# The first two projections of a hybrid trunk made side by side, from weights stored in the order of their use

## The chip, the cores and the metric

The kernel runs on one core of a Trainium2 chip. The metric is device time in microseconds; three runs of the kernel before took 2539.45, 2540.48 and 2542.24 us (median 2540.48). PE is TensorE (products), PEld its loads of weights, DVE is VectorE, ACT ScalarE, POOL GpSimd; SP is the engine that issues transfers.

## What is computed

The reference is a trunk of two layers on 256 tokens of width 2048: differential attention and a gated MLP with a short convolution, then a gated delta rule and a second MLP. The change touches the start of the attention:

```python
h = rms_norm(x, mixer_norm[0])
qkv = h @ w_qkv                      # 2048 x (2048 q, 2048 k, 2048 v)
q = rms_norm(q.reshape(..., 16, 128), q_norm) * 128 ** -0.5
k = rms_norm(k.reshape(..., 16, 128), k_norm)
...                                  # 8 heads, each of two halves of 128
```

All is float32, and must stay close to it.

## The kernel before

Everything lies transposed: `x` is 16 tiles of 128 features by 256 tokens (k = 0 to 15). A float32 number is carried as a sum of two parts that PE multiplies fast, hi (rounded to float32r) and lo (the rest). `weights` (line 75) fetches a piece of a weight matrix into a buffer `raw` (the transfer is issued by SP), ACT casts it to `whi` (line 86) and DVE subtracts to get `wlo` (line 87). There are four buffers of each, with room for 128 x 1024 numbers. `norm_tile` (line 184) makes the activations of one k likewise: ACT multiplies by the gain and rounds (line 189), DVE makes the rest (line 190). The division by the norm comes later, from a sum of squares, `norm_stat`.

`dense` (line 98) makes one block: 256 columns of the output, as two column tiles of 128, over all 16 k. It fetches 4 k at a time (512 KB); for each k and column tile it issues a pair of products: hi of the weights with both parts of the activations (512 wide, line 117) and lo of the weights with hi of the activations (256 wide, line 118). A block of 16 k is thus 32 pairs. It accumulates in one large PSUM tile `ps` of two banks per column tile pair; there are two such tiles, `banks`, and four small tiles of a bank each, `mp`.

`attention` (line 348) makes a block of q and a block of k for each of eight heads, in turn: q of head 0, k of head 0, q of head 1, and so on. The first block is special: its activations don't exist yet, so `start` (line 971) makes them as they are asked for, and issues the transfers of x on the way, and its first piece holds a single k (`lead`). A block of q or k is merged from its two parts out of PSUM by `normed` (line 387, `merge` at 143), and background work (sums of squares, statistics, weights of the attention, written as generators) goes forward by one step at each `tick`, that is after each piece. A scheduler then moves instructions of each engine past each other where no data forbid it.

Ahead of all this stand 18 products of a 128 x 128 tile of ones with itself (line 953), whose result is not used. The gains come by a transfer of their own (line 940).

Of the kernel before, what the change touches and what calls it, by code (L numbers as in the profile page):

```python
# [8 lines left out]
F32 = mybir.dt.float32  # L9
# [12 lines left out]
CK = 4  # L22
WARM = 18
LNEXP = "natural_log_exp_and_others"


class Trunk:
# [8 lines left out]
    def __init__(self, ctx, tc):  # L36
# [37 lines left out]

    def weights(self, ap):

        nc = self.nc
        nk, n = ap.shape[1:]

        def tile_(tag, dt, bufs):  # L80
            t = self.wp.tile([P, CK * T], dt, tag=tag, name=tag, bufs=bufs)
            return t[:, :nk * n].rearrange("p (k n) -> p k n", n=n)

        raw, hi, lo = tile_("raw", F32, 4), tile_("whi", F32R, 4), tile_("wlo", F32R, 4)
        self.loaded = nc.sync.dma_start(raw, ap)
        self.cast = nc.scalar.copy(hi, raw)  # L86
        nc.vector.tensor_tensor(lo, raw, hi.bitcast(F32), ALU.subtract)  # L87
        return hi, lo

    def chunks(self, kt, ck, first=0):  # L90

        c = [(k, min(ck, kt - k)) for k in range(0, kt, ck)]
        return [(0, first), (first, c[0][1] - first)] + c[1:] if first else c

    def banks(self):
        return self.dps.tile([P, 2, 2 * T], F32, tag="ps", name="ps")

    def dense(self, w, kt, acts, tiles=2, lead=0, wide=True, each=None):
# [6 lines left out]
        for k0, nk in self.chunks(kt, CK, lead):  # L105
            hi, lo = self.weights(w[:, k0:k0 + nk, :])
# [14 lines left out]
            self.tick()  # L121
        return ps

# [19 lines left out]
    def merge(self, ps, u, pool=None, scaled=True):  # L143

        nc = self.nc
        n = u.shape[1]
        main, small = self.halves(ps[:, :n])
        v = "p c (q j) -> p c q j"
# [198 lines left out]

    def attention(self, w_qk, w_v, w_o, nh, dist_ap, ident_ap, qg, kg, lvec, sub, start, done, lambda_init):

        nc, mp = self.nc, self.mp  # L350
        with self.tc.tile_pool(name="at", bufs=1) as at:
            self.spawn(self.norm_stat(4, at))
            qgs = at.tile([P, 1], F32, tag="qgs", name="qgs")
# [7 lines left out]
            def prepare():  # L361
                for _ in range(5):
                    yield
# [104 lines left out]
            for h in range(nh):  # L468
                acts, lead = (self.h_acts, 0) if h else (start, 1)
                qn, go = normed(self.dense(w_qk[h], KD, acts, lead=lead), qgs)  # L470
                self.spawn(go)
                kn, go = normed(self.dense(w_qk[nh + h], KD, self.h_acts), kg)
# [393 lines left out]
def _layout(inputs):  # L866
# [30 lines left out]
    for t, n in ((0, P), (1, T)):  # L897
# [8 lines left out]
        np.concatenate([_tiles(x["ffn_conv_w"][i].reshape(-1)), _tiles(x["ffn_conv_b"][i])], 1).reshape(P, 4, 2, NJ)  # L906
        for i in range(2)]
    def turned(w):
        return w.reshape(*w.shape[:-1], T, 2).swapaxes(-1, -2).reshape(w.shape)

    out = {
        "x": x["x"][0].T.reshape(KD, P, T).transpose(1, 0, 2),
        "cols": np.concatenate(col, 1),
        "w_qk": blocks(x["diff_w_qkv"][0], KD, pairs(2 * NH)),
        "w_v": turned(blocks(x["diff_w_qkv"][0], KD, [[(2 * NH * T + T * h, 2 * T)] for h in range(0, NH, 2)])),
# [18 lines left out]
def trunk_kernel(tc, a, out):  # L934
    nc = tc.nc
    with ExitStack() as ctx:
        t = Trunk(ctx, tc)
        n = a["cols"].shape[1]
        cols = t.cp.tile([P, n], F32, tag="cols", name="cols")
        nc.sync.dma_start(cols[:, :KD], a["cols"][:, :KD])  # L940
        parts = t.chunks(KD, CK, 1)

        def load():
            if parts:
                k, n = parts.pop(0)
                nc.sync.dma_start(t.x[:, k:k + n, :], a["x"][:, k:k + n, :])

# [4 lines left out]
        for _ in range(WARM):  # L952
            nc.tensor.matmul(warm[:, :P], t.onesr, t.onesr, start=True, stop=True)

# [16 lines left out]
        def start(k):  # L971

            if len(begun) <= k:
                if k == 0 or k in starts:
                    load()
                if k == KD - 1:
                    with tc.issue_after(t.loaded.ins):
                        nc.sync.dma_start(cols[:, KD:], a["cols"][:, KD:])
                then(mixer, 0)(k)
                begun.append(k)  # L980
            return t.h[k]

        t.attention(a["w_qk"], a["w_v"], a["w_o"], NH, a["dist"], a["const"][:, :P], qg, kg, lvec, sub, start, then(ffn, 0),
                    0.8 - 0.6 * math.exp(-0.3 * 0))
# [20 lines left out]
```

## Time and profile before

| | |
|---|---|
| median of three runs | 2540.48 us |
| the profiled execution | 2540.85 us |
| its span, first to last instruction | 2539.0 us |
| PE busy | 2530.1 us |
| DVE, ACT, POOL busy | 1899.5, 1506.3, 91.5 us |
| read from memory | 482.31 MB, 191 GB/s over the span |

A row of a timeline gives the start (us from the start of the span), how long it took, the engine, the line of the kernel, the operation, what it writes and reads, the shape, and in brackets how long the engine stood idle ahead of it and what ended that. A row of waits gives who waited for whom, us in total, times, and the longest. Products overlap: one that is listed with 0.38 us may be followed by the next after 0.22 us, so the distance between starts is the measure.

### The profile page before, as it was taken

The numbers are of one execution on the slowest core, as the hardware profiler recorded it, in microseconds if no ns is written. First come the engines' busy times: TensorE is split into PE (matmuls) and PEld (weight loads), VectorE is DVE, ScalarE is ACT, GpSimd is POOL, SyncE is SP. The second block draws the span as 40 slices with busy tenths as digits, with TensorE's granted clock in tenths as the row PEclk, the third lists the DMA queues.
The fourth block names the chain that finished last, engine by engine and source line by source line (L and its number), as shares of the span: only waits on it lengthen the run. The fifth ranks groups of instructions, "written<-read, shape, count | busy, mean of one in ns | idle before, by whom it ended". The sixth has DMA issues, their size and how long they took to land.

```text
span 2539.0 us, 44069 instructions
## 1 busy us (share of the span) xinstructions
PE 2530.1 (100%) x17442; PEld 2360.4 (93%) x17442; DVE 1899.5 (75%) x2787; ACT 1506.3 (59%) x2073; POOL 91.5 (4%) x189
## 2 busy tenths in 40 slices
PE   9999999999999999999999999999999999999999
PEld 8998899999999999999999999999999999999998
DVE  8876678777777555689878788788787777776544
ACT  7666556666666444485674674674566666665443
POOL 0000000000000000010121011021000000000000
PEclk9999999999999999999999999999999999999999
DMA  7555566666666666666555555555466666666665
GB/s 246 176 183 176 170 201 201 202 200 201 201 201 201 201 199 201 203 189 200 164 168 191 165 183 176 175 182 177 159 200 201 202 201 200 201 201 207 207 208 156
DMA packets 137775, 487.33 MB, mean 192 GB/s; under 512 B 15552, under 2 KB 18784, under 8 KB 137568
## 3 DMA queue, kind: packets, MB, share of 16 engines
q1 hardware_dynamic: 137280, 484.16, 60.5%
q8 instruction: 137, 2.24, 0.4%
q14 instruction: 70, 0.57, 0.1%
q10 hardware_dynamic: 288, 0.35, 0.0%
HBM read 482.31 MB, written 2.15 MB: 191 GB/s over the span
## 4 chain that ended last, share of the span: by engine, by line
PE 99%; DMA 1%; DVE 0%; ACT 0%; SPq 0%; issue 0%
PE ps L117 48%; PE ps L118 27%; PE ps L120 7%; PE ps L175 3%; PE ps L176 3%; PE ps L177 3%; PE mp L700 2%; PE mp L117 1%; PE mp L284 1%; PE mp L573 1%; PE mp L118 0%; PE mp L665 0%; PE mp L683 0%; PE mp L745 0%; PE mp L451 0%; PE mp L421 0%
## 5 line engine op out<-in xcount | busy, mean ns | idle before, releaser
L87 DVE TENSOR_TENSOR wlo<-raw,whi 128x1024 fp32r<-128x1024 f32 (+2 forms) x909 | 1103.1, 1215 | 520.3 <-ACT whi L86 512.1
L86 ACT CAST whi<-raw 128x1024 fp32r<-128x1024 f32 (+2 forms) x909 | 944.2, 1040 | 867.8 <-PE ps L117 558.1
L117 PE MATMUL ps<-h,whi 128*128 128x512 f32 (+1 forms) x4304 | 1361.6, 357 | 1.4 <-ACT whi L86 1.4
L118 PE MATMUL ps<-h,wlo 128*128 128x256 f32 x4304 | 1179.5, 274 | 0.6 <-DVE wlo L87 0.6
L117 PEld LDWEIGHTS ps<-h,whi 128*128 128x128 f32 x4304 | 819.7, 190 | 87.0 <-ACT whi L86 2.0
L118 PEld LDWEIGHTS ps<-h,wlo 128*128 128x128 f32 x4304 | 827.7, 192 | 2.5 <-DVE wlo L87 1.4
L117 PE MATMUL ps<-ac,whi 128*128 128x512 f32 x1546 | 506.8, 382 | 0.0
L118 PE MATMUL ps<-ac,wlo 128*128 128x256 f32 x1546 | 421.5, 273 | 0.0
L117 PEld LDWEIGHTS ps<-ac,whi 128*128 128x128 f32 x1546 | 293.1, 190 | 40.1 <-PE ps L117 0.2
L118 PEld LDWEIGHTS ps<-ac,wlo 128*128 128x128 f32 x1546 | 297.0, 192 | 0.1
L120 PE MATMUL ps<-h,whi 128*128 128x256 f32 x1040 | 287.5, 277 | 0.0
L120 PEld LDWEIGHTS ps<-h,whi 128*128 128x128 f32 x1040 | 199.9, 192 | 0.4
L175 PE MATMUL ps<-whi,h 128*128 128x512 f32 x384 | 146.4, 381 | 0.0
L177 PE MATMUL ps<-whi,h 128*128 128x512 f32 x384 | 146.2, 381 | 0.0
L176 PE MATMUL ps<-wlo,h 128*128 128x512 f32 x384 | 146.2, 381 | 0.0
L265 DVE SCALAR_TENSOR_TENSOR cv<-u,fcols,cv 128x255 f32<-128x255 f32 (+1 forms) x344 | 142.7, 477 | 0.0
L117 PE MATMUL ps<-oc,whi 128*128 128x256 f32 x512 | 142.5, 278 | 0.0
L120 PE MATMUL ps<-oc,whi 128*128 128x256 f32 x512 | 142.1, 278 | 0.0
L118 PE MATMUL ps<-oc,wlo 128*128 128x256 f32 x512 | 141.7, 277 | 0.0
L120 PEld LDWEIGHTS ps<-oc,whi 128*128 128x128 f32 x512 | 98.3, 192 | 0.3
L118 PEld LDWEIGHTS ps<-oc,wlo 128*128 128x128 f32 x512 | 98.4, 192 | 0.2
L117 PEld LDWEIGHTS ps<-oc,whi 128*128 128x128 f32 x512 | 98.4, 192 | 0.1
(208 smaller groups left out, 2151.2 us busy)
## 6 DMA issues: line engine op xcount, KB each, us to landing
raw<-w_up SPq DMA_DIRECT2D x344, 512.0 KB, 4.8
raw<-w_down SPq DMA_DIRECT2D x160, 512.0 KB, 3.8
raw<-w_in SPq DMA_DIRECT2D x128, 512.0 KB, 4.6
raw<-w_z SPq DMA_DIRECT2D x64, 512.0 KB, 4.0
raw<-w_out SPq DMA_DIRECT2D x64, 512.0 KB, 4.2
raw<-w_qk SPq DMA_DIRECT2D x63, 512.0 KB, 4.6
raw<-w_v SPq DMA_DIRECT2D x32, 512.0 KB, 3.9
raw<-w_o SPq DMA_DIRECT2D x32, 512.0 KB, 4.7
```

Source lines behind the costliest of these rows:

```text
L86: self.cast = nc.scalar.copy(hi, raw)
L87: nc.vector.tensor_tensor(lo, raw, hi.bitcast(F32), ALU.subtract)
L117: nc.tensor.matmul(bank[c][:, :n], hi[:, k, s], self.turns(a[:, :n // T, :]), start=first, stop=False)
L118: nc.tensor.matmul(bank[c][:, :T], lo[:, k, s], self.turns(a[:, :1, :]), start=False, stop=last and wide)
L120: nc.tensor.matmul(bank[c][:, :T], hi[:, k, s], self.turns(a[:, 1:, :]), start=False, stop=last)
L175: nc.tensor.matmul(ps[:, c, :], ah, wh, start=first, stop=False)
L176: nc.tensor.matmul(ps[:, c, :], ah, wl, start=False, stop=False)
L177: nc.tensor.matmul(ps[:, c, :], al, wh, start=False, stop=last)
L265: nc.vector.scalar_tensor_tensor(out[:, j:], u[:, :T - j], taps[n - 1 - j], out[:, j:], ALU.mult, ALU.add)
L284: last = self.nc.tensor.matmul(out, self.onesr, self.pairs(p[:, j]), start=i + j == 0, stop=i + j == n)
L573: nc.tensor.matmul(p[:, P:384], k[:, :P], r, start=True, stop=True)
L700: nc.tensor.matmul(p[:, v, :], l(v), r[:, v, :], start=i == 0, stop=i == len(terms) - 1)
```

## The change

Four things are changed, all at the start.

**The first two blocks side by side.** `dense_two` makes q and k of head 0 together in the two large PSUM tiles: for each k four pairs, two for q and two for k, so each activation is used at once for both. Their weights are stored anew, as `w_first`: for k = 0 to 11 the columns of q and k stand next to each other, 512 for each k, behind them the last four k of q, and the last four of k. They come in pieces of one k for k = 0 to 3 (two such pieces share one buffer), of two k up to 11, and then the last quarter of each block. The piece of k = 0 is cast in two halves.

**Transfers.** x comes in eight pieces of two k in place of five; the gains are stored in front of x, in one tile with it, and come with its first piece.

**The products of ones.** Seven in place of 18, each 512 wide in place of 128 (the tile of ones is read four times over).

**The third block.** q of head 1 goes into two small PSUM tiles in place of a large one (`apart`), and is merged in two halves. The statistics of the norm are begun after 8 steps of the background in place of 4, the small constants after 10 in place of 5.

```diff
-WARM = 18
+WARM = 7
...
-        self.x = self.cp.tile([P, KD, T], F32, tag="x", name="x")
+        self.gx = self.cp.tile([P, KD + KD * T], F32, tag="x", name="x")
+        self.x = self.gx[:, KD:].rearrange("p (k t) -> p k t", t=T)
...
+    def weights(self, ap, parts=1, slots=None, at=0):
...
+        for i in range(parts):
+            s = slice(i * n // parts, (i + 1) * n // parts)
+            self.cast = nc.scalar.copy(hi[:, :, s], raw[:, :, s])
+            nc.vector.tensor_tensor(lo[:, :, s], raw[:, :, s], hi[:, :, s].bitcast(F32), ALU.subtract)
...
+    def firsts(self):
+        return [(k, 1) for k in range(4)] + self.chunks(KD, 2)[2:]
+
+    def dense_two(self, w, acts, done):
+        ps = [self.banks(), self.banks()]
+        cut = KD - CK
+        parts = [(c, (0, 1)) for c in self.firsts() if c[0] < cut] + [((cut, CK), (b,)) for b in range(2)]
+        at = 0
+        for (k0, nk), bs in parts:
+            for k in range(nk):
+                acts(k0 + k)
+            n = len(bs) * T
+            ap = w[:, at:at + nk * n].rearrange("p (k n) -> p k n", n=n)
+            at += nk * n
+            if nk == 1 and k0 % 2 == 0:
+                slots = self.slots()
+            hi, lo = self.weights(ap, 1 if k0 else 2, slots if nk == 1 else None, k0 % 2 * 2 * T if nk == 1 else 0)
+            for i, b in enumerate(bs):
+                for c in range(2):
+                    s = slice(i * T + c * P, i * T + (c + 1) * P)
+                    for k in range(nk):
+                        a = acts(k0 + k)
+                        first, last = k0 + k == 0, k0 + k == KD - 1
+                        nc.tensor.matmul(ps[b][:, c, :], hi[:, k, s], self.turns(a), start=first, stop=False)
+                        nc.tensor.matmul(ps[b][:, c, :T], lo[:, k, s], self.turns(a[:, :1, :]), start=False, stop=last)
+                if k0 == cut:
+                    done[b](ps[b])
+            self.tick()
...
-        ps = self.banks() if each is None else None
-        bank = [self.mp() if each else ps[:, c] for c in range(tiles)]
+        ps = None if each or apart else self.banks()
+        bank = [ps[:, c] if ps else self.mp() for c in range(tiles)]
...
+        if isinstance(ps, list):
+            for c in range(2):
+                k = slice(c, c + 1)
+                main, small = self.halves(ps[c].unsqueeze(1))
+                nc.scalar.copy(t[:, k].rearrange(v, q=2), small)
+                nc.vector.tensor_tensor(u[:, k].rearrange(v, q=2), main, t[:, k].rearrange(v, q=2), ALU.add)
...
-            self.spawn(self.norm_stat(4, at))
+            self.spawn(self.norm_stat(8, at))
...
-                for _ in range(5):
+                for _ in range(10):
...
-        nc.sync.dma_start(cols[:, :KD], a["cols"][:, :KD])
-        parts = t.chunks(KD, CK, 1)
+        parts = t.chunks(KD, 2)
...
-            nc.tensor.matmul(warm[:, :P], t.onesr, t.onesr, start=True, stop=True)
+            nc.tensor.matmul(warm, t.onesr, t.onesr.unsqueeze(1).to_broadcast([P, 4, P]), start=True, stop=True)
```

The order of the instructions shows three places. First the transfers that SP issues from the start of the program, before (x_76 is x, each raw a weight buffer; the shapes are those in SBUF):

```order
L940 DMA cols_81<-cols 128x16
L946 DMA x_76<-x 128x256
L85 DMA raw_113<-w_qk 128x256
L946 DMA x_76<-x 128x768
L85 DMA raw_127<-w_qk 128x768
L946 DMA x_76<-x 128x1024
L85 DMA raw_152<-w_qk 128x1024
```

and now:

```order
L1003 DMA x_76<-x 128x528
L86 DMA raw_104<-w_first 128x512 x2
L1003 DMA x_76<-x 128x512
L86 DMA raw_137<-w_first 128x512 x2
L1003 DMA x_76<-x 128x512
L86 DMA raw_169<-w_first 128x1024
L1003 DMA x_76<-x 128x512
L86 DMA raw_196<-w_first 128x1024
```

For each k now 256 KB of weights come with 128 KB of x, where before it was 128 with 128; the small transfer of the gains is gone from the head of the queue.

Second the work of ACT over the same stretch, before:

```order
L189 ACTIVATE h_77<-x_76,cols_81 128x256
L86 CAST whi_114<-raw_113 128x256
L189 ACTIVATE h_77<-x_76,cols_81 128x256 x3
L86 CAST whi_128<-raw_127 128x768
L189 ACTIVATE h_77<-x_76,cols_81 128x256 x4
L86 CAST whi_153<-raw_152 128x1024
```

and now, up to the piece of k = 10 and 11 (raw_250):

```order
L234 ACTIVATE h_77<-x_76 128x256 x2
L89 CAST whi_105<-raw_104 128x256 x2
L89 CAST whi_105<-raw_104 128x512
...
L89 CAST whi_138<-raw_137 128x512 x2
...
L89 CAST whi_170<-raw_169 128x1024
...
L89 CAST whi_197<-raw_196 128x1024
...
L89 CAST whi_224<-raw_223 128x1024
L234 ACTIVATE h_77<-x_76 128x256 x6
L89 CAST whi_251<-raw_250 128x1024
```

Two activations stand ahead of each of the pieces up to k = 9, then the last six stand together ahead of the cast of k = 10 and 11.

Third, on PE, where the third block (q of head 1) begins, before (ps_255 is the tile of the second block, ps_380 that of the third):

```order
L117 MATMUL ps_255<-h_77,whi_351 128x512
L117 MATMUL ps_380<-h_77,whi_382 128x512
L118 MATMUL ps_255<-h_77,wlo_352 128x256
...
L118 MATMUL ps_380<-h_77,wlo_383 128x256
L117 MATMUL ps_380<-h_77,whi_382 128x512
```

and now (ps_101 is the tile of k of head 0, mp_349 and mp_350 the two small tiles):

```order
L124 MATMUL ps_101<-h_77,wlo_317 128x256
L151 MATMUL mp_349<-h_77,whi_352 128x512
L151 MATMUL mp_350<-h_77,whi_352 128x512
L419 MATMUL mp_413<-lp_96,ones_72 128x2
L152 MATMUL mp_349<-h_77,wlo_353 128x256
L152 MATMUL mp_350<-h_77,wlo_353 128x256
```

The third block begins behind the whole of the second, and the small product for lambda (L374 before, L419 now) has moved from the middle of the first block to the head of the third.

More of the change, by code (lines that the diff above doesn't have):

```diff
@@ L73, in tick, with slots @@
                 self.bg.remove(g)
-    def weights(self, ap):
+    def slots(self):
+        return [self.wp.tile([P, CK * T], dt, tag=tag, name=tag, bufs=4)
+                for tag, dt in (("raw", F32), ("whi", F32R), ("wlo", F32R))]
+    def weights(self, ap, parts=1, slots=None, at=0):
         nc = self.nc
         nk, n = ap.shape[1:]
[L80 to L84, printed above, removed]
+        raw, hi, lo = (t[:, at:at + nk * n].rearrange("p (k n) -> p k n", n=n) for t in slots or self.slots())
@@ L907, in _layout @@
         for i in range(2)]
+    qk = blocks(x["diff_w_qkv"][0], KD, [[(T * (h + i), T)] for h in range(NH) for i in (0, NH)])
+    two, cut = qk[:2], KD - CK
     def turned(w):
```

53 lines of the change are left out of this document (33 added, 20 removed).

## The prediction, made before the changed kernel ran

> **What bounds the kernel now.** The page comes first: the busy times and the chain that ended last.
>
> ```profile
> span 2539.0 us, 44069 instructions
> PE 2530.1 (100%) x17442; PEld 2360.4 (93%) x17442; DVE 1899.5 (75%) x2787; ACT 1506.3 (59%) x2073; POOL 91.5 (4%) x189
> PE 99%; DMA 1%; DVE 0%; ACT 0%; SPq 0%; issue 0%
> ```
>
> PE is busy for 2530.1 of 2539.0 us. An edit can only gain by taking products away, by running them at a higher clock, or by closing the few holes. The view of waits, for PE over the whole span, says where the holes are:
>
> ```profile
> PE mp L284 <- DVE qp L277: 1.5, 1, 1.5
> PE ps L117 <- ACT whi L86: 1.4, 1, 1.4
> PE mp L953 <- DVE onesr L54: 1.3, 1, 1.3
> PE ps L118 <- DVE wlo L87: 0.6, 2, 0.4
> ```
>
> All but the first (in the delta-rule stage, which the change doesn't touch) lie in the first 14 us. There the timeline of PE shows a second loss that no wait shows:
>
> ```profile
> 1.31 4.10 PE L953 MATMUL mp<-onesr 128*128 128x128 f32 x18 [1.31 <-DVE onesr L54]
> 5.95 0.64 PE L117 MATMUL ps<-h,whi 128*128 128x512 f32 x1
> 8.25 0.80 PE L117 MATMUL ps<-h,whi 128*128 128x512 f32 x1 [1.45 <-ACT whi L86]
> ...
> 9.61 0.64 PE L117 MATMUL ps<-h,whi 128*128 128x512 f32 x1
> 10.25 0.64 PE L117 MATMUL ps<-h,whi 128*128 128x512 f32 x1
> ...
> 11.96 0.31 PE L118 MATMUL ps<-h,wlo 128*128 128x256 f32 x1
> ...
> 13.19 0.38 PE L118 MATMUL ps<-h,wlo 128*128 128x256 f32 x1 [0.37 <-DVE wlo L87]
> ...
> 31.44 0.38 PE L117 MATMUL ps<-h,whi 128*128 128x512 f32 x1
> 31.77 0.38 PE L117 MATMUL ps<-h,whi 128*128 128x512 f32 x1
> ```
>
> A pair is one 512-wide product with hi (L117) and one 256-wide with lo (L118). Until 11.96 pairs start 0.64 us apart (9.61, 10.25); later they start 0.33 apart (31.44, 31.77; 0.328 as a mean). So PE ran at half speed until 11.96, though the clock column prints full speed for those slices. The products of ones from 1.31 to 5.41 did not lift it.
>
> The first two blocks, q and k of head 0, are 64 pairs, or 64 x 0.328 = 21.0 us at full speed. Sixty-four pairs' worth is done at 31.77. One thing in that time is not head loss, the small product on lambda:
>
> ```profile
> 18.41 0.38 PE L117 MATMUL ps<-h,whi 128*128 128x512 f32 x1
> 18.63 0.28 PE L374 MATMUL mp<-lp,ones 128*128 128x2 f32 x2
> 18.89 0.38 PE L118 MATMUL ps<-h,wlo 128*128 128x256 f32 x1
> ```
>
> It takes 18.89 - 18.63 = 0.26 us, and the change moves it behind the second block. The comparable time is 31.77 - 0.26 = 31.5 us. The head loses 31.5 - 21.0 = 10.5 us, and this is all that the change can touch: from the output projection on, the order of every engine is the same in both programs.
>
> **Removed and added.** Eighteen narrow products become seven wide ones. Both stand ahead of the first product on data. A 512-wide product at half speed holds PE for 0.43 us (an estimate: two thirds of the 0.64 of a pair), so the seven end at 1.31 + 7 x 0.43, about 4.4, where the old ones end at 5.41. Nothing of this is on the path unless data are there by then. What the width does to the clock is weighed below.
>
> When data are there depends on the transfers. Their landings are read from what ACT waited for, and their rate from the stretches of the windows view (last two columns: DMA share, GB/s):
>
> ```profile
> 3.42 0.51 ACT L189 ACTIVATE h<-x,cols 128x256 fp32r<-128x256 f32 x1 [1.41 <-DMA x<-x]
> 3.84 0.40 ACT L86 CAST whi<-raw 128x256 fp32r<-128x256 f32 x1
> 5.97 1.31 ACT L189 ACTIVATE h<-x,cols 128x256 fp32r<-128x256 f32 x3 [1.73 <-DMA x<-x]
> 7.36 0.83 ACT L86 CAST whi<-raw 128x768 fp32r<-128x768 f32 x1
> 9.23 1.71 ACT L189 ACTIVATE h<-x,cols 128x256 fp32r<-128x256 f32 x4 [1.04 <-DMA x<-x]
> 10.84 1.03 ACT L86 CAST whi<-raw 128x1024 fp32r<-128x1024 f32 x1
> ...
> 17.45 0.61 ACT L212 ACTIVATE q<-x 128x512 f32<-128x512 f32 x1
> ```
>
> ```profile
> 2.30:7.40 5.10, 4.50 (x19) 3.90 (x18) 1.71 (x5) 2.17 (x6) 0.00 (x0) 1.00 0.96 262
> ...
> 9.20:14.00 4.80, 4.39 (x17) 3.65 (x18) 3.78 (x8) 4.77 (x10) 0.00 (x0) 1.00 1.03 415
> 14.20:15.40 1.20, 1.20 (x10) 1.10 (x9) 1.20 (x3) 1.20 (x4) 0.00 (x0) 1.00 1.03 390
> ```
>
> The queue lands its transfers in order. Sums in KB: 136 by 3.42, 264 by 3.84, 648 by 5.97, 1032 by 7.36, 1544 by 9.23, then about 400 GB/s, or 390 KB/us. The stretch from 14.20 holds the 1252-byte rows of the columns and still moves 390 GB/s, so I take rows of 2 KB for no slower. The first transfer is also issued sooner, since the gains now travel with x:
>
> ```profile
> 0.73 0.38 SPq L940 DMA_DIRECT2D cols<-cols  x1
> 1.17 0.42 SPq L946 DMA_DIRECT2D x<-x  x1
> ```
>
> That is 0.44 us. By the same curve less 0.44, the new order lands: x0,1 with the gains (264 KB) 3.4; weights of k=0 4.9, of k=1 6.0; x2,3 6.9; weights of k=2 7.9, of k=3 8.8; x4,5 9.5; weights of k=4,5 (2312 KB) 10.8; of k=6,7 12.7; of k=8,9 14.7; the six x behind 16.6; weights of k=10,11 18.0; the two last quarters 19.7 and 21.0. There are more transfers, but SP issues one each 0.47 us, ahead of all these landings.
>
> ACT makes hi and the activations, DVE makes lo:
>
> ```profile
> L87 DVE TENSOR_TENSOR wlo<-raw,whi 128x1024 fp32r<-128x1024 f32 x3 | 3.7, 1222 | 0.5 <-ACT whi L86 0.5
> L87 DVE TENSOR_TENSOR wlo<-raw,whi 128x768 fp32r<-128x768 f32 x1 | 1.0, 957 | 0.4 <-ACT whi L86 0.4
> L87 DVE TENSOR_TENSOR wlo<-raw,whi 128x256 fp32r<-128x256 f32 x1 | 0.4, 419 | 0.0
> ```
>
> Casts take 0.40 (256 wide) and 1.03 (1024); a 512-wide one is not in the trace of before, its nearest row is the 0.61 of L212; lo of that width lies between 0.42 and 0.96, say 0.68. Activations follow each other in 1.71 / 4 = 0.43. So hi of k=0 is there at 4.9 + 0.4 = 5.3, lo at 5.75; k=1 6.6 and 7.3; k=2 8.5 and 9.2; k=3 9.4 and 10.1; k=4,5 11.8 and 13.0; k=6,7 13.7 and 15.1; k=8,9 15.7 and 17.1. Then six activations stand ahead of the cast of k=10,11: 15.75 + 6 x 0.43 = 18.3, hi 19.4, lo 20.6. The last quarters have lo at 22.0 and 24.3.
>
> At full speed PE has k=0 to 3 done by 11.5 and waits for k=4,5: lo at 13.0. Behind that stand 48 pairs, 15.7 us, less the two hi products that the order puts ahead of the first lo (0.44): **28.3**. No later piece is late: PE wants lo of k=10,11 at 20.9 (there at 20.6), the quarters at 23.3 and 25.9.
>
> If the clock is still low, at full rate only from F, the end is F + (64 - (F - 5.5) / 0.64) x 0.328 = 0.49 F + 23.8. It passes 28.3 only if F is over 9.2. Before, the clock rose 11.96 - 8.25 = 3.7 us into the first unbroken stretch of wide products. Counted from the new first product at 5.4 that gives F = 9.1, still 28.3; at twice that delay F = 12.8 and the end 30.0. I take 28.5, a little above the earlier end.
>
> The Trainium skill, "TensorE: Matmul & The Clock Gate", part 1, says the clock is lifted after one window of about 3.4 us of sustained matmuls, in windows that run freely. The trace agrees in the 3.7 us from 8.25, and not for the narrow products: PE's rows are unbroken for 4.1 us from 1.31, and the rate stays low. By the page, the seven wide ones would give F between 4.7 and 8.1 and the sum 28.3; if they count for nothing, up to 12.2 and 29.8.
>
> **Third block.** Both large PSUM tiles are taken by the first two, so it goes into two small ones; merging them takes two half copies on ACT and two half sums on DVE. By the 256-wide rows that is 0.8 in place of about 0.6 on each. ACT then stands idle for over a microsecond at a time (1.57 ahead of the cast at 43.33), so it costs nothing; 0.2 us if that cover were gone. The statistics of the norm move from pair 75 to pair 96, and products of the head sums wait for them in PE's order:
>
> ```profile
> 36.33 1.28 ACT L252 ACT_TABLE_LOAD   x1 [0.69 <-PE mp L237]
> ...
> 43.33 1.05 ACT L86 CAST whi<-raw 128x1024 fp32r<-128x1024 f32 x1 [1.57 <-PE ps L117]
> ...
> 46.88 0.69 DVE L277 TENSOR_TENSOR sqp<-sq,sqp 128x512 fp32r<-128x512 f32 x1
> ```
>
> From the statistics' release of ACT to the first split square took 47.6 - 36.3 = 11.3 us. In the new order the product that needs this square stands 37 pairs, some 12.4 us, behind them: a cover of about 1 us. I take nothing; a microsecond is the upper end.
>
> **The sum.** 31.5 - 28.5 = 3.0 us less. The profiled execution took 2540.85 us (1.85 around its span), 0.4 above the median of the three runs: 2540.85 - 3.0 = 2537.9, or from the median 2540.48 **2537.5 us**, 0.12% less. About 0.2%, 5.1 us, is what a measurement of this kernel can tell from no change.
>
> **Rivals.** *The clock stays low* to F of 11 to 15, because the ones and the pause behind them count for nothing: third block at 29.2 to 31.1, 2538 to 2540. For it: the narrow ones counted for nothing before. Against it: a 512-wide product leaves no gap for the weight load. *The start of the transfers is quicker.* If 415 GB/s held from the first landing, ACT's own work would be the limit: from 3.4, six activations, five casts and the one of k=4,5 are 6 x 0.43 + 2 x 0.40 + 3 x 0.61 + 1.03 = 6.2, with lo 10.9, and 15.3 behind it 26.2: 5.3 us less, 2535.2. For it: only the first 7 us are slow, and other addresses are read. Against it: nothing in the edit speeds the queue itself. *Slower:* the new rows, 2 KB with a stride of 32 KB, hold the queue to its early rate. From 264 KB at 3.4, 6.2 MB at 262 GB/s land at 27.0, and with 1.0 + 1.2 + 2.4 us behind it the third block starts at 31.7, as before. This decides from about 265 GB/s; at 217 GB/s it starts at 36.6, 5.1 us later, 2545.6. Against it: 390 GB/s with 1252-byte rows. That the change does not run side by side at all is excluded by the order of PE.
>
> **How the numbers follow.** Forecast (2536.8 to 2538.3) 0.52; low clock 0.23; quicker transfers 0.19; slow transfers 0.06. The range takes in most of the low clock and the quicker transfers: 2534.9 to 2540.1. Faster by over 0.2%: 0.17, nearly all of the third case; slower by over 0.2%: 0.04, most of the last; within: 0.79.
>
> **What would show it.** In the profile after: the ones end near 4.4; pairs 0.33 apart by 9; PE's waits in the first 14 us on lo of k=4,5; the first product of the third block near 28.5 (30 or more: low clock; under 27: transfers); ACT's cast of k=4,5 at 10.8; no new wait of PE between 30 and 60. The forecast is wrong if that first product is where I say and the time is not, or the other way round.

## The result, and the profile after

| | before | after |
|---|---|---|
| median (21 runs of each, side by side) | 2540.85 us | 2536.93 us |
| lowest and highest | 2538.99, 2543.51 us | 2535.64, 2538.76 us |
| the profiled execution | 2540.85 us | 2537.79 us |
| its span | 2539.0 us | 2536.1 us |
| first product of the third block (before: its 65th wide product with hi) | 31.77 us | 28.80 us |

The ratio is 0.9986, with an interval of 0.998 to 0.9991: 3.9 us or 0.15% less. So the time did fall (1 lies outside the interval), and the gain is within the 0.2% that the prediction called no change that can be told. Forecast were 2537.5 us, 3.0 us less, and a third block at 28.5.

The page of the changed kernel, in the three lines that were shown of the kernel before:

```profile
span 2536.1 us, 44059 instructions
...
PE 2527.5 (100%) x17431; PEld 2354.5 (93%) x17431; DVE 1898.8 (75%) x2790; ACT 1505.4 (59%) x2076; POOL 91.6 (4%) x189
...
PE 99%; DMA 1%; DVE 0%; ACT 0%; SPq 0%; issue 0%
```

PE is busy 2.6 us less in a span that is 2.9 us shorter: what went was products running at half speed, which count as busy, and 0.75 us of ones (4.10 before, 3.35 now), and only a little idle time. The view of PE's waits over the whole span agrees; its columns are us in total, times, longest:

```profile
PE mp L329 <- DVE qp L322: 1.6, 1, 1.6
PE mp L1010 <- DVE onesr L55: 1.3, 1, 1.3
PE ps L123 <- DVE h L235: 0.8, 1, 0.8
PE ps L124 <- DVE wlo L90: 0.6, 1, 0.6
PE ps L123 <- ACT whi L89: 0.5, 2, 0.3
```

The waits in the head add up to 1.9 us behind the ones (0.8, 0.6, 0.5) against 2.0 before. The first row, in the delta-rule stage, stands as it stood (1.5 before). The timeline of PE shows the order of the head's events:

```profile
1.31 3.35 PE L1010 MATMUL mp<-onesr 128*128 128x512 f32 x7 [1.31 <-DVE onesr L55]
4.87 0.79 PE L123 MATMUL ps<-h,whi 128*128 128x512 f32 x2 [0.20 <-ACT whi L89]
...
6.87 0.38 PE L123 MATMUL ps<-h,whi 128*128 128x512 f32 x1
...
7.20 0.38 PE L123 MATMUL ps<-h,whi 128*128 128x512 f32 x1
...
9.22 0.70 PE L123 MATMUL ps<-h,whi 128*128 128x512 f32 x2 [0.77 <-DVE h L235]
...
13.41 0.38 PE L124 MATMUL ps<-h,wlo 128*128 128x256 f32 x1 [0.56 <-DVE wlo L90]
...
28.80 0.60 PE L151 MATMUL mp<-h,whi 128*128 128x512 f32 x2
```

The ones end at 4.66. Pairs are 0.33 apart already at 6.87 and 7.20, where before they were 0.64 apart until 11.96. PE then waits for k = 2 (9.22) and for lo of k = 4,5 (13.41), and from there runs without a gap into the third block, 28.80 - 13.41 = 15.39 us on. The kernel before waits for the last time in the head at almost the same moment, 13.19, also for a lo of k = 4 (the row is in the prediction). But by then it has started 8 products with lo, and the changed kernel 16: the data of k = 0 to 3 feed twice as many pairs. Eight pairs at 0.328 us are 2.6 us, most of the 2.97 between 31.77 and 28.80. What the changed kernel's lo of k = 4,5 waits for is read from ACT:

```profile
7.76 0.91 ACT L234 ACTIVATE h<-x 128x256 fp32r<-128x256 f32 x2 [1.37 <-DMA x<-x]
...
11.04 1.06 ACT L89 CAST whi<-raw 128x1024 fp32r<-128x1024 f32 x1 [0.38 <-DMA raw<-w_first]
```

ACT stands idle for the weights of k = 4,5 until they land at 11.02, so that it is the queue that sets this chain here, and not ACT. It does so by 0.38 us only: weights that landed sooner by more than that would find ACT still at work. The queue's rate is in the view of windows (last two columns: DMA share, GB/s):

```profile
2.30:7.40 5.10, 4.59 (x16) 3.00 (x15) 2.25 (x5) 2.12 (x5) 0.00 (x0) 1.00 0.92 305
9.20:14.00 4.80, 4.19 (x22) 3.19 (x23) 3.96 (x7) 4.26 (x8) 0.00 (x0) 1.00 1.03 402
```

It is slow in the first 7 us, as before (262 there), and moves 402 GB/s behind, with rows of 2 and 4 KB, where the kernel before moved 415.

### The profile page after: what moved, and what is told of

It is laid out like the page before. It is cut to its first block, busy times and chain, and to the rows that moved or that the text cites. A ratio compares the mean times of both kernels' runs of the same rounds, so it can differ in the third digit from the quotient of the medians.

```text
span 2536.1 us, 44059 instructions
## 1 busy us (share of the span) xinstructions
PE 2527.5 (100%) x17431; PEld 2354.5 (93%) x17431; DVE 1898.8 (75%) x2790; ACT 1505.4 (59%) x2076; POOL 91.6 (4%) x189
## 4 chain that ended last, share of the span: by engine, by line
PE 99%; DMA 1%; DVE 0%; ACT 0%; SPq 0%; issue 0%
PE ps L151 47%; PE ps L152 27%; PE ps L154 7%; PE ps L220 3%; PE ps L221 3%; PE ps L222 3%; PE mp L752 2%; PE mp L151 1%; PE mp L329 1%; PE mp L625 1%; PE mp L152 0%; PE ps L123 0%; PE mp L717 0%; PE mp L735 0%; DMA raw<-w_first 0%; PE mp L797 0%
## 5 line engine op out<-in xcount | busy, mean ns | idle before, releaser
L151 PE MATMUL ps<-h,whi 128*128 128x512 f32 (+1 forms) x4208 | 1327.0, 356 | 0.0
L152 PE MATMUL ps<-h,wlo 128*128 128x256 f32 x4208 | 1151.0, 274 | 0.0
L151 PEld LDWEIGHTS ps<-h,whi 128*128 128x128 f32 x4208 | 798.3, 190 | 83.6
L152 PEld LDWEIGHTS ps<-h,wlo 128*128 128x128 f32 x4208 | 807.7, 192 | 0.9
L154 PEld LDWEIGHTS ps<-h,whi 128*128 128x128 f32 x1040 | 199.5, 192 | 0.4
```

Source lines behind the costliest of these rows:

```text
L151: nc.tensor.matmul(bank[c][:, :n], hi[:, k, s], self.turns(a[:, :n // T, :]), start=first, stop=False)
L152: nc.tensor.matmul(bank[c][:, :T], lo[:, k, s], self.turns(a[:, :1, :]), start=False, stop=last and wide)
L154: nc.tensor.matmul(bank[c][:, :T], hi[:, k, s], self.turns(a[:, 1:, :]), start=False, stop=last)
```

## The experiments

The theory: the head's end is set by the landing of the weights of k = 4,5, then cast, lo, and 48 pairs at full speed; the gain is that of the side-by-side order, which brings the weights as PE uses them. Rivals: the higher clock carries the gain (by the wide ones), the smaller pieces carry it, or ACT and DVE set the end and not the queue. Each diff is against the kernel named.

### The changed kernel again

> The changed kernel once more. If the gain is head loss alone, the third block begins within 0.7 us of the 28.80 of the first profile, the clock rises within 1 us of 4.7, and the time is 2.7 to 4.5 us below before. If the 1.0 us between the two profiles' difference (2.9) and the medians' (3.9) is something that only some executions show, this profile and the times should again differ by about that.

Measured: 2536.72 us, ratio 0.9985 [0.9976, 0.9994]. Its timeline of PE:

```profile
12.74 0.38 PE L124 MATMUL ps<-h,wlo 128*128 128x256 f32 x1 [0.56 <-DVE wlo L90]
...
28.13 0.60 PE L151 MATMUL mp<-h,whi 128*128 128x512 f32 x2
```

The weights of k = 4,5 landed at 10.36, 0.66 sooner than in the first profile; lo came 0.67 sooner and the third block 0.67 sooner. Landing to lo is 2.38 to 2.39 us, and lo to third block 15.39, in both. One thing fell outside what was expected: the clock rose at 6.01, 1.3 us later than in the first profile. The span is 3.8 us below that of the kernel before, as much as the medians, so the 2.9 of the first pair of profiles was not the rule. The same 15.39 was found in every run below with this wait in it and the third block in small tiles behind whole first blocks (12.99 to 28.38, 13.26 to 28.65, 13.17 to 28.56).

### The changed kernel with narrow ones

```diff
-WARM = 7
+WARM = 18
...
-            nc.tensor.matmul(warm, t.onesr, t.onesr.unsqueeze(1).to_broadcast([P, 4, P]), start=True, stop=True)
+            nc.tensor.matmul(warm[:, :P], t.onesr, t.onesr, start=True, stop=True)
```

> The changed kernel with the 18 narrow products of ones. My theory (data decide, the clock is worth little): pairs 0.64 us apart until some point between 9 and 13 us, third block between 28.8 and 30.1, time 0 to 1.3 us above the changed kernel, so 2.6 to 3.9 below before. Rival (the early clock carries the gain): third block at 31 or later, within 1 us of before.

Measured: 2536.92 us, ratio 0.9984 [0.9975, 0.9993], the same as the changed kernel. PE:

```profile
8.46 0.64 PE L123 MATMUL ps<-h,whi 128*128 128x512 f32 x1
...
9.11 0.64 PE L123 MATMUL ps<-h,whi 128*128 128x512 f32 x1
...
29.83 0.38 PE L151 MATMUL mp<-h,whi 128*128 128x512 f32 x1
```

Pairs stay 0.64 apart; the trace's record of the granted clock rises at 11.75. Yet the third block begins only 1.0 to 1.7 us later: while PE ran slowly it used up waits that it has at full speed (it never waits for lo of k = 4,5 here). The rule of the prediction, 0.49 F + 23.8 with F the time from which PE runs at full rate, gives 29.6 for F = 11.75. This profiled execution was the slowest of its eleven (2538.59 us, 1.7 above their median), so the usual cost is less. By the starts of this execution the wide ones are worth 1.0 to 1.7 us, by the medians 0.2 us or less, and the gain does not hang on them.

### The kernel before with wide ones alone

The same edit the other way round, in the kernel before.

> The kernel before with the seven wide products of ones and nothing else changed. My theory: the clock rises near 4.7, but PE waits again for lo of k=4 to 7 at 13.1, so the third block stays within 0.3 us of 31.8 and the time within 0.5 us of before. Rival (the early clock carries the gain): third block at 29.5 or earlier, 2 us or more below before.

Measured: 2540.41 us, ratio 0.9998 [0.999, 1.0007]: no gain. PE, then the windows of the same run (the column ahead of the last two is the granted clock):

```profile
5.07 0.38 PE L117 MATMUL ps<-h,whi 128*128 128x512 f32 x1
...
8.06 0.79 PE L117 MATMUL ps<-h,whi 128*128 128x512 f32 x1 [2.50 <-ACT whi L86]
...
9.42 0.64 PE L117 MATMUL ps<-h,whi 128*128 128x512 f32 x1
...
10.06 0.64 PE L117 MATMUL ps<-h,whi 128*128 128x512 f32 x1
...
31.98 0.38 PE L117 MATMUL ps<-h,whi 128*128 128x512 f32 x1
```

```profile
4.23:7.64 3.41, 1.24 (x6) 0.60 (x4) 1.70 (x5) 1.69 (x5) 0.00 (x0) 1.00 0.96 293
7.64:14.47 6.83, 6.21 (x18) 4.96 (x19) 5.68 (x12) 5.92 (x13) 0.00 (x0) 0.50 1.02 412
```

The clock rose with the ones (4.23), and the two pairs that had data ran at full speed. Then PE had nothing to do for 2.50 us, and the clock fell back at 7.64 for 6.83 us: the pairs from 9.42 on are 0.64 apart. The forecast of no gain held, but by a way that I had not thought of: the old order of the transfers leaves a hole in which an early clock was lost again. The wide ones do not carry the gain without the new order.

### The kernel before with small pieces alone

```diff
-        return [(0, first), (first, c[0][1] - first)] + c[1:] if first else c
+        return [(0, first), (1, 1)] + [(k, 2) for k in range(2, kt, 2)] if first else c
...
-        parts = t.chunks(KD, CK, 1)
+        parts = t.chunks(KD, 2)
```

The steps of the background are counted anew for the larger number of pieces.

> The kernel before, its first block still by itself, but its pieces small: weights of k=0 and 1 apart, then two k, x by two k (the background's steps counted anew). Theory A (side by side is what gains, since each k then feeds four pairs, 1.31 us of PE against 0.98 us of transfer, where one block has 0.66 against 0.66): third block at 30.8 or later, less than 1 us gained. Theory B (the size of the pieces is what gains, since PE no longer waits for 1024-wide casts): third block between 28.8 and 30, 1.5 to 3 us gained.

Measured: 2541.84 us, ratio 1.0007 [0.9998, 1.0015]: no gain. The waits of SP up to 21 us, then PE:

```profile
SPq L85 <- DVE wlo L87: 5.3, 6, 1.3
```

```profile
22.43 0.38 PE L118 MATMUL ps<-h,wlo 128*128 128x256 f32 x1 [0.78 <-DVE wlo L87]
...
33.13 0.38 PE L117 MATMUL ps<-h,whi 128*128 128x512 f32 x1
```

Product 32 starts at 20.82, 0.25 sooner than before (21.07), but the third block later, at 33.13 for 31.77. A small piece takes a whole one of four buffers here, so SP waits for a buffer (5.3 us in six waits) and the later weights come late. So small pieces in the old order bring nothing. That they would with larger room in the buffers is not excluded by this run; the run with two k to a piece, below, bounds it from the other side.

### The changed kernel with an extra transfer

```diff
+        late = slice(KD + 14 * T, KD + 16 * T)
+        nc.sync.dma_start(t.gx[:, late], a["x"][:, late])
```

> The changed kernel with 256 KB more ahead in the queue: the two tiles x14,15 are loaded right behind the first transfer, and a second time at their old place. What is computed is the same. Theory (the landing of the weights of k=4,5, then its cast and lo, set where the third block begins): 256 KB at 262 to 400 KB/us put off every later landing by 0.65 to 1.0 us, the wait on lo of k=4,5 moves from 12.7 or 13.4 to 13.4 to 14.4, and the third block begins at 28.8 to 29.8, each 15.4 us behind that lo; the time goes up by 0.6 to 1.0 us beside the changed kernel. Rival (the casts and activations of ACT or the sums of DVE set it, not the landings): the third block begins at 28.1 to 28.8, as without.

Measured: 2537.76 us, ratio 0.9989 [0.998, 0.9998]. PE:

```profile
6.11 1.22 PE L123 MATMUL ps<-h,whi 128*128 128x512 f32 x2 [1.44 <-ACT whi L89]
...
29.35 0.60 PE L151 MATMUL mp<-h,whi 128*128 128x512 f32 x2
```

The third block falls into the theory's bounds, but not by the theory's way, and the run does not tell the two apart. The weights of k = 0 landed at 5.63, 1.4 us later than in the two profiles above (4.17 and 4.25), but those of k = 4,5 at 11.16, only 0.14 behind the first profile (0.80 behind the second). The first stretch moved 306 GB/s, as in those two (305 and 306), and why 256 KB more cost so little by then stays open. What decided was the clock. The first product came at 6.11, 1.44 us behind the ones, the clock rose only at 10.59, and PE never waited for lo of k = 4,5. From 6.11 at 0.64 a pair and from 10.59 at 0.328, 64 pairs end at 10.59 + (64 - 7.0) x 0.328 = 29.3. This is the low-clock rival of the prediction, seen on the chip. The profiled execution was the slowest of its ten. By the medians the gain is 2.6 us where the changed kernel had 3.8 to 4.0, so the extra transfer cost 1.1 to 1.4 us for the 0.6 to 1.0 expected.

### Single pieces up to k = 7

```diff
-        return [(k, 1) for k in range(4)] + self.chunks(KD, 2)[2:]
+        return [(k, 1) for k in range(8)] + self.chunks(KD, 2)[4:]
```

> The changed kernel with the pieces of one k carried on to k=7 instead of k=3, so that hi and lo of k=4 are made as soon as its own 256 KB are there. Theory: the wait of PE on lo of k=4,5 (0.56 us) goes, since lo of k=4 is there 0.5 us and one half cast sooner; the third block begins 0.4 to 0.6 us sooner beside the landing of the weights of k=4 and 5, at 27.6 to 28.4, and the time goes down by about 0.5 us, too little to measure. Rival (PE is then late on something else, on k=2 and 3 or on the two pieces of k=6,7 whose casts cost 0.2 us more together): the wait shows up again at another k and the third block begins at 28.1 to 28.8.

Measured: 2537.39 us, ratio 0.9988 [0.9979, 0.9997]. PE, then ACT, then DVE:

```profile
24.40 0.38 PE L124 MATMUL ps<-h,wlo 128*128 128x256 f32 x1 [1.30 <-DVE wlo L90]
```

```profile
15.99 0.63 ACT L257 ACTIVATE s<-x 128x512 f32<-128x512 f32 x1
...
21.44 1.03 ACT L89 CAST whi<-raw 128x1024 fp32r<-128x1024 f32 x1
```

```profile
21.73 0.68 DVE L259 TENSOR_TENSOR s<-s,q 128x512 f32<-128x512 f32 x1
22.34 0.87 DVE L235 SCALAR_TENSOR_TENSOR h<-x,h 128x256 fp32r<-128x256 f32 x2
23.13 1.22 DVE L90 TENSOR_TENSOR wlo<-raw,whi 128x1024 fp32r<-128x1024 f32 x1
```

The wait on lo of k = 4,5 is gone, as expected, and a longer one has taken its place at 24.40, on lo of a last quarter. Its cast ends at 22.47, but DVE is busy until 23.13 with a sum of the norm's statistics (line 259) and its part of two activations (line 235). The edit moved more than it meant to: more pieces mean more ticks, so the squares of the statistics (line 257) begin at 15.99 on ACT, where the changed kernel has them at 21.08. The 65th wide product starts at 29.30 (two products of the third block slip in at 27.12). My theory had 27.6 to 28.4 and fell. The rival was right that the wait would show up at another k, but it looked for it at k = 2,3 or 6,7 and had the price too low. What single pieces would do with the statistics held in place was not tried.

### The third block in a large tile

```diff
-                        pair.append(normed(self.dense(w_qk[2 * h - 2 + i], KD, self.h_acts, apart=h + i == 1), g))
+                        pair.append(normed(self.dense(w_qk[2 * h - 2 + i], KD, self.h_acts, apart=False), g))
```

> The changed kernel with the third block in the large PSUM tiles, as the blocks behind it. Theory: both large tiles are taken by the first two blocks, which end together, so the first product of the third block waits until the half of the first tile has been merged; the merge of the first block ends some 0.5 to 1.0 us behind its last product, so PE waits 0.5 to 1.0 us there, on DVE, and the time goes up by as much, too little to measure. Rival (the scheduler or the merge is early enough, the small tiles bring nothing): no wait of PE between 27 and 31, and the third block begins at 28.1 to 28.8.

Measured: 2537.44 us, ratio 0.9989 [0.998, 0.9998]. PE:

```profile
12.63 0.38 PE L124 MATMUL ps<-h,wlo 128*128 128x256 f32 x1 [0.53 <-DVE wlo L90]
...
28.14 0.27 PE L124 MATMUL ps<-h,wlo 128*128 128x256 f32 x1
28.84 0.48 PE L151 MATMUL ps<-h,whi 128*128 128x512 f32 x1 [0.43 <-DVE qkr L200]
```

PE waits for the merge of the first block (line 200). Without it the first product would follow 0.11 behind the last lo, at 28.25, so the stall is 0.59 us: as the theory had it. (From lo to the third block it is 16.21 us for 15.39. The other 0.23 us is the small product for lambda, which stands at 20.60 here, inside the first two blocks.) The small tiles save the stall, in a kernel whose median moves too little to show it.

### One narrow product of ones

```diff
-        for _ in range(WARM):
-            nc.tensor.matmul(warm, t.onesr, t.onesr.unsqueeze(1).to_broadcast([P, 4, P]), start=True, stop=True)
+        for _ in range(1):
+            nc.tensor.matmul(warm[:, :P], t.onesr, t.onesr, start=True, stop=True)
```

> The changed kernel with a single narrow product of ones in place of seven wide ones. Theory (the clock is nearly free, since the data of k=4,5 bound the head): pairs start 0.64 us apart until 8 to 12 us, the third block begins at 28.1 to 29.8 by the greater of lo of k=4,5 plus 15.4 and 0.49 F + 23.8, F being where the pairs become 0.33 apart; the time goes up by 0 to 1 us, not to be measured. Rival (the wide ones carry the gain): the clock stays low beyond 15 us, or falls back, the third block begins at 31 or later and the time is within 1 us of that of the kernel before.

Measured: 2537.27 us, ratio 0.9989 [0.998, 0.9997]. PE:

```profile
4.91 1.22 PE L123 MATMUL ps<-h,whi 128*128 128x512 f32 x2 [3.12 <-ACT whi L89]
...
8.13 0.38 PE L123 MATMUL ps<-h,whi 128*128 128x512 f32 x1
...
12.99 0.38 PE L124 MATMUL ps<-h,wlo 128*128 128x256 f32 x1 [0.55 <-DVE wlo L90]
...
28.38 0.60 PE L151 MATMUL mp<-h,whi 128*128 128x512 f32 x2
```

With PE idle until 4.91 the clock still rises at 8.02, below the 9.2 from which the prediction had it matter, PE still waits for lo of k = 4,5, and the third block begins where the data let it. In this execution the ones were worth nothing.

### Two k to a piece from the first

```diff
-        return [(k, 1) for k in range(4)] + self.chunks(KD, 2)[2:]
+        return self.chunks(KD, 2)
```

> The changed kernel with two k to a piece from the first one, instead of one k to a piece for k=0 to 3. Theory (the side-by-side blocks gain, since PE gets two pairs' work for each KB of x and the weights come in order of use; the small first pieces only start PE sooner, and lo of k=4,5 decides): the first product on data moves from 4.9 to about 6.3 to 7, and the third block begins at 28.1 to 29.8, within 1 us of the changed kernel. Rival (the small pieces carry the gain): the third block begins at 30.5 or later, and half of the gain or more is lost.

Measured: 2537.93 us, ratio 0.9989 [0.998, 0.9998]. PE:

```profile
5.75 1.00 PE L123 MATMUL ps<-h,whi 128*128 128x512 f32 x2 [1.19 <-ACT whi L89]
...
10.78 0.38 PE L124 MATMUL ps<-h,wlo 128*128 128x256 f32 x1 [0.56 <-DVE wlo L90]
...
29.18 0.38 PE L151 MATMUL mp<-h,whi 128*128 128x512 f32 x1
```

Two points came otherwise than the theory had them. The first product on data starts at 5.75, sooner than the 6.3 expected, and the last long wait, at 10.78, is for lo of k = 2,3 and not of k = 4,5, with 8 pairs done where the changed kernel has 16 at 13.41. The third block begins 0.4 to 1.05 us later than in the changed kernel, and by the medians the time is 1.2 us longer than in the run of the changed kernel beside it (2536.69, below), a little over what the theory allowed. The rival had 30.5 or later. So by the starts 2.6 of 3.2 us of the gain stand without the single pieces (31.75 - 29.18, and 31.75 - 28.53 as means), by the medians 2.7 of 4.0.

### The kernel before again, and where the rest of the time differs

> The kernel before, once more, for the spread of its own profile. Theory (the head and the wait at 1107 us are all that differs between executions): product 65 of the first two blocks' count starts between 31.5 and 33, the wait in the delta-rule stage is 0.3 to 1.8 us, and the span less the two is within 0.2 us of that of the first profile. If the median gain of 3.6 to 3.9 us in place of 2.9 comes from the head, product 65 starts nearer to 32.5 than to 32.1; the rival, that it comes from elsewhere, has the head at 32.1 and a rest that is longer.

Measured: 2540.88 us, ratio 1.0001 [0.9991, 1.001]. The waits of PE, and its timeline:

```profile
PE mp L284 <- DVE qp L277: 0.8, 1, 0.8
```

```profile
31.74 0.38 PE L117 MATMUL ps<-h,whi 128*128 128x512 f32 x1
```

Two things come of it. By the trace's record its clock rose at 13.65, 1.6 us later than in the first profile (12.02), and the 65th product still starts at 31.74 for 31.77: the early clock was worth nothing in the kernel before either. The expectation looked for the missing part of the median gain in the head or in the rest, and found it in neither: the head is that of the first profile (31.77 there, where the expectation wrote 32.1) and so is the rest. And the wait in the delta-rule stage is 0.79 us for 1.53. All profiled executions can be put side by side (us; the wait is PE's at 1105 to 1114; rest is the span less the two):

| kernel | clock rises | 65th product | wait | span | rest |
|---|---|---|---|---|---|
| before | 12.02 | 31.77 | 1.53 | 2539.0 | 2505.7 |
| before again | 13.65 | 31.74 | 0.79 | 2538.2 | 2505.7 |
| after | 4.73 | 28.80 | 1.56 | 2536.1 | 2505.7 |
| after again | 6.01 | 28.13 | 1.51 | 2535.2 | 2505.6 |
| narrow ones | 11.75 | 29.83 | 1.43 | 2536.9 | 2505.6 |
| before, wide ones | 4.23, 14.47 | 31.98 | 1.13 | 2538.8 | 2505.7 |
| before, small pieces | 12.99 | 33.13 | 1.10 | 2539.9 | 2505.7 |
| extra transfer | 10.59 | 29.35 | 1.81 | 2536.9 | 2505.7 |
| single pieces to 7 | 4.27 | 29.30 | 0.68 | 2535.6 | 2505.6 |
| large tile | 5.82 | 28.84 | 0.28 | 2534.8 | 2505.7 |
| one narrow one | 8.02 | 28.38 | 1.23 | 2535.4 | 2505.8 |
| two k to a piece | 4.32 | 29.18 | 1.16 | 2536.1 | 2505.8 |
| addition on POOL, missed | 6.55 | 28.65 | 1.21 | 2535.4 | 2505.5 |
| first addition on POOL | 5.49 | 28.56 | 1.11 | 2535.2 | 2505.5 |

The rest is the same to 0.3 us in fourteen executions. What the variants do to the span is in the third column, and what is left between executions is in the fourth.

### The wait that is left, at 1105 us

The wait at 1105 is no part of the change, but it blurs each comparison, and its cause could be tried. DVE of the changed kernel there:

```profile
1105.15 0.69 DVE L610 TENSOR_TENSOR lt<-lt,con 128x512 f32<-128x512 f32 x1 [2.97 <-DMA lt<-grow]
1105.76 0.68 DVE L322 TENSOR_TENSOR qp<-qs,qp 128x512 fp32r<-128x512 f32 x1
```

PE needs line 322; DVE stands for a DMA out of DRAM, for line 610 ahead of it. In the run with the large tile the DMA came at 1103.79, and the wait was 0.28. A first attempt put line 610 on POOL under a condition that did not hold:

```diff
+                adder = nc.gpsimd if d is None else nc.vector
...
-                nc.vector.tensor_tensor(dv, dv, m4, ALU.add)
+                adder.tensor_tensor(dv, dv, m4, ALU.add)
```

> The changed kernel with one addition of the delta-rule stage (that of the mask to the first pair's gate rows, the one that waits for a DMA from DRAM) on POOL instead of DVE. Theory: the time that is left between executions of one program comes from the landing of this DMA at 1103.8 to 1105.2 us, behind which the split of the next pair's squares stands in DVE's order, so that PE waits 0.3 to 1.8 us at 1105; with the addition on POOL the split no longer stands behind it, the wait at 1105 us falls below 0.3 us, and what follows the start of the third block takes 2505.5 to 2506 us instead of 2506.0 to 2507.4; the time goes down by 0.5 to 1.5 us. Rival (PE is next late on the gate rows themselves or on ACT's exponentials, which now come behind the slower engine): the wait shows up again within 10 us behind, as large or larger, and the time stays or goes up.

All sixteen additions stayed on DVE, so this was the changed kernel a third time: 2536.69 us, ratio 0.9985 [0.9976, 0.9994], a wait of 1.21 us. The second attempt:

```diff
-                nc.vector.tensor_tensor(dv, dv, m4, ALU.add)
+                (nc.gpsimd if hq == 0 else nc.vector).tensor_tensor(dv, dv, m4, ALU.add)
```

> The changed kernel with the addition of the mask to the gate rows of the first pair of heads on POOL instead of DVE (line 610, the one that waits for a DMA from DRAM and stands in DVE's order directly ahead of the split of the next squares; the edit before this one left it on DVE, since its condition did not hold for it). Theory: the wait of PE of 0.3 to 1.8 us at 1105 us (on the split, line 322) is DVE standing still for this DMA; with the addition on POOL the wait on line 322 at 1105 us goes to nothing, since the cast ahead of the split ends at 1101.4 us; the stretch from product 17200 to product 10000 counted from the end takes 1161.3 to 1161.8 us instead of 1161.9 to 1163.1, and the time goes down by 0.3 to 1.5 us. Rival (PE is next late on the gate rows themselves or on ACT's exponentials behind the slower engine): a wait of the same size shows up within 20 us behind, and the stretch takes 1162 us or more.

Measured: 2537.09 us, ratio 0.9983 [0.9974, 0.9992]: no faster than the changed kernel. POOL, then PE's waits behind 14 us:

```profile
1105.36 1.27 POOL L610 TENSOR_TENSOR lt<-lt,con 128x512 f32<-128x512 f32 x1 [46.98 <-DMA lt<-grow]
```

```profile
PE ps L152 <- DVE wlo L90: 0.9, 1, 0.9
PE ps L151 <- ACT whi L89: 0.2, 1, 0.2
```

The wait on line 322 is gone, so it was DVE standing for this DMA. In its place PE waits 0.20 us at 1113.05 and 0.91 at 1114.33, for weights whose casts ACT now makes behind its exponentials (line 616, from 1106.67, the addition on POOL taking 1.27 us for 0.69). The rival held: 1.1 us in place of 1.2 to 1.6. The stretch that I had named, up to product 10000 from the end, can't be used, as the order of PE moved there; the table's rest shows the same.

## Why the prediction was right, point by point

**The bound.** The chain named was the one that decided: landing of the weights of k = 4,5, cast, lo, 48 pairs. Forecast 10.8, 13.0, 28.3, with 28.5 taken; the three executions of the changed program gave 11.02, 13.41, 28.80, then 10.36, 12.74, 28.13, and 10.87, 13.26, 28.65, a mean of 28.53 for the third block. That the mean lies 0.03 from the forecast is luck, as single executions lie up to 0.4 us from it; that the chain of terms holds in each of them is not. Landing to lo was forecast as 2.2 and is 2.4; lo to third block 15.3 and is 15.39. That the queue set it and not ACT is read from ACT: in each of the eight executions with single pieces up to k = 3 it stood idle for 0.37 or 0.38 us ahead of that cast, until the landing. The two experiments meant to part the two (the extra transfer, single pieces up to k = 7) did not do it.

**The sum.** The head was to fall from 31.5 to 28.5. With the small product on lambda left where each program has it, it falls from 31.75 (two executions) to 28.53, 3.2 us; with its 0.26 us taken off the first, as the prediction did, 3.0. The rest in the table is no longer where it holds that product, so at this precision the deduction is not borne out. The spans of these executions differ by 3.0 (2538.6 and 2535.6 as means), and the medians by 3.9, in an interval of 2.3 to 5.1 us. Most of the 0.9 us between is which executions were profiled. The spans of all executions are on record: 118 of the kernel before have a mean of 2538.8, 43 of the changed one 2535.2, so 3.6 us, with single executions 0.7 to 0.8 us (standard deviation) about these means. So the prediction was right in its path and, by these spans, some 0.6 us low in size; of that the third block's start accounts for 0.2, and how the rest divides is not shown.

**The ones and the clock.** The ones end at 4.66 for 4.4. Their starts lie 0.43 us apart, as forecast, but the first takes 0.59 until the next starts, and the last one's own 0.63 us counts to its end. The pause behind them (0.20 us) is shorter than forecast, since k = 0 landed at 4.17 and not 4.9. The clock rose at 4.73, 6.01 and 6.55, not at 9.1. This step was wrong, and cost nothing, because the prediction had it matter only above 9.2: the runs at 11.75 and 10.59 show the third block at 29.83 and 29.35, in the rival's 29.2 to 31.1, and the run at 8.02 shows no loss. The Trainium skill, "TensorE: Matmul & The Clock Gate", part 1, has the clock lifted after a window of about 3.4 us of sustained matmuls, from which the prediction estimated 4.7 to 8.1 for the wide ones, and the rises at 4.73, 6.01 and 6.55 agree.

**The transfers.** Of the landings forecast, k = 1 (6.0) came at 5.58 to 6.88 and x of k = 2,3 (6.9) at 7.07 to 7.73. The second is the row at 9.22 where PE waits 0.77 us for h; I had not named that wait. It is absorbed, since PE waits 0.56 us for lo of k = 4,5 behind it in any case; up to 0.56 us more of it would have been free. Neither the quicker nor the slower transfers came true: 305 GB/s at first and 402 behind it, for the 262 and 415 of before. The prediction's bound for the slower case, 265 GB/s, is the rate at which nothing is gained; by its own terms the queue would set the end below some 305 GB/s already (3.4 + 6.2 MB / 305 + 4.6 = 28.3).

**The third block and the statistics.** Costed at nothing, upper end a microsecond (37 pairs are 12.1 us and not 12.4, so the cover was 0.8). No wait of PE over 0.15 us lies between 14 and 1100 us in the profile of the changed kernel. The large tile would have cost 0.59 us.

**Which part gains.** The wide ones alone bring nothing, small pieces alone bring nothing; without wide ones, without small PSUM tiles or without single pieces the changed kernel keeps 2.7 us or more by the medians (2.7, 2.9, 3.1, 3.6 in the four runs). What is left is the order of the first two blocks with weights in the order of their use. The count of pairs at the last wait shows how it gains: 8 started at 13.19 before, 16 at 12.63 to 13.41 in the six runs with the new order that wait for lo of k = 4,5. It was not run with all the rest undone at once, so that the other parts add nothing is by elimination. The pieces of x, the gains carried with them and the later statistics were not undone one by one.

## What to carry to other kernels

When PE is busy all the time, look at the distance between products, not at busy time: the head's loss was 10 us, of which the waits showed 3.3. Find the one landing behind which PE never stops again, and count from there; earlier waits and a late clock are then free up to a point that can be worked out. And put the gain together from the place where two programs start to be equal: here one row (the 65th product) and one wait gave every span to 0.3 us, where 21 runs gave 3.9 with an interval of 2.3 to 5.1.

## What the runs showed of the hardware

The clock falls back. With the ones wide in the old order it rose at 4.23, PE was busy for 1.24 of the next 3.41 us, and it fell for 6.83 us, twice 3.41. In the run with two k to a piece it rose at 4.32 too, and a pause of 1.19 us behind the ones did not make it fall. The Trainium skill, "TensorE: Matmul & The Clock Gate", part 1, has the clock drop after an idle window of about 3.4 us; here a window with a third of it busy was idle enough.

Unbroken products are not all alike: 18 of 128 columns (4.10 us) left the clock low in four executions (rises at 12.02, 13.65, 11.75, 12.99), with seven of 512 columns (3.2 to 3.4 us) it rose between 4.23 and 6.55 in eight of nine. In the ninth 1.44 us of idle time followed the ones, and it rose at 10.59. Chance in the phase of the windows does not explain the narrow ones away. The recorded steps lie whole multiples of 3.413 us apart (3.41 and 6.83 in the run above, 740 to 742 times 3.413 from the rise to the fall at the end in the other traces). Counted back by that from 12.02 and 11.75, the stretches 1.78 to 5.19 and 1.51 to 4.92 lay wholly within the narrow products and did not lift the clock. The narrow ones start 0.213 us apart and the wide ones, with four times the columns, 0.427: by this estimate columns fill only half of the narrow ones' time. That this is the reason is not shown.

The first 7 us of the queue differ between executions by up to 1.3 us at the same landing (k = 1 at 5.58 to 6.88 in one program), with 286 to 306 GB/s for the 400 that follow; a quarter of a megabyte more there put off k = 0 by 1.2 to 1.5 us, and k = 4,5 by 0.1 to 0.8.
